# Other start bytes for the pools of on-chip tiles in a hybrid decoder block (short convolution, RG-LRU, MLP)

## The chip, the core and the metric

The kernel runs on one core of a Trainium2 chip. The metric is the device time of one execution in microseconds (us); a lower number is better.

## What is computed

One decoder block over a sequence of 2048 tokens of 1024 features, in fp32:

```
h = rmsnorm(x, norm_mix_g)
u = h @ w_in                                    # 1024 -> 3584 columns
gate_b, gate_c, v, x_r, g = split(u)            # 512, 512, 512, 1024, 1024 columns
y_conv = gate_b * causal_dwconv(gate_c * v, conv_w)         # 3 taps
xr = causal_dwconv(x_r, rnn_conv_w) + rnn_conv_b            # 4 taps
y_rnn = rg_lru(xr, w_a, b_a, w_x, b_x, lru_lambda) * gelu(g)
y = concat(rmsnorm(y_conv, g_norm_conv), rmsnorm(y_rnn, g_norm_rnn))
x = x + y @ w_out                                           # 1536 -> 1024
z = square(relu(rmsnorm(x, norm_mlp_g) @ w_mlp_in))         # 1024 -> 4096
x = x + z @ w_mlp_out                                       # 4096 -> 1024
out = rmsnorm(x, final_norm_g)
```

`rg_lru` makes two sigmoid gates by 64-wide block-diagonal products and runs a linear recurrence along the tokens.

## The kernel before

**Tiling.** The tokens are cut into four blocks of 512 (`TB`), and the features into chunks of 128 partitions. Blocks are handled in pairs: the mixers and the output projection of block 0, then those of block 1, then the MLP of both together; the same again for blocks 2 and 3. The MLP of a pair is done by a scheme with seven products in place of eight (classes `Up` and `Down`, order `ORDER`), whose intermediate `z` tiles are written to device memory and fetched again.

**Products.** Each fp32 operand is split into a high part of type fp32r and the rest, also fp32r: ScalarE casts the high part (`split_into`, L153), VectorE subtracts it (L154). Each product is then three TensorE matmuls: high by high, high by low, low by high. Nearly all matmuls take 128x128 stationary columns and a moving operand of 512 columns. These are the places:

| line | product | stationary operand, its pool | moving operand, its pool | names in the profile |
|---|---|---|---|---|
| L193 | `h @ w_in` | weights, `wp` | h, `hp` | ps_g, ps_x, ps_b, ps_c, ps_v |
| L213 | `y @ w_out` | y, `tp` | weights, `wp` | po |
| L584 | gates of the RG-LRU | gates, `tp` | xr, `tp` | psri |
| L731 | `Up` of the MLP | weights, `wp` | H, `tp` (H1 and H2 in `hp`) | up |
| L845 | `Down` of the MLP | z, `wp` | weights, `wp` | dn |

L420 is the first product of the program, on 256 moving columns. L976 are transposes of 128x128 in fp32 against the identity `ident`.

**Pools.** All tiles lie in SBUF pools, opened in this order:

```
    cp = ctx.enter_context(tc.tile_pool(name="cp", bufs=1))
    hp = ctx.enter_context(tc.tile_pool(name="hp", bufs=2))
    tp = ctx.enter_context(tc.tile_pool(name="tp", bufs=TSLOTS))
    wp = ctx.enter_context(tc.tile_pool(name="wp", bufs=WSLOTS))
    xp = ctx.enter_context(tc.tile_pool(name="xp", bufs=2))
    sp = ctx.enter_context(tc.tile_pool(name="sp", bufs=4))
```

`cp` holds constants and parameters. `hp` has two tiles of 16384 bytes per partition for h. `tp` has 29 general tiles (`TSLOTS`) of 4096 bytes, `wp` 15 tiles (`WSLOTS`) of 4096 bytes for weights and their parts (and for the parts of `z`). `xp` has two tiles of 4128 bytes for `xr_in` and `cv`, the inputs of the convolutions, which take turns. `sp` holds small columns. The pools lie one behind the other in a partition, so the size of `cp` sets where all others begin. Since 4096 and 16384 are multiples of 512, all tiles of a pool lie at the same byte of a 512-byte block; of the two tiles of `xp` the second lies 32 bytes further on.

**Order.** A layer records the instructions and puts them into the queues of the engines with their waits; some stretches are in the order in which they are written (`manual_schedule`). SyncE issues all DMAs. The order does not look at addresses.

Of the kernel before, what the change touches and what calls it, by code (L numbers as in the profile page):

```python
# [8 lines left out]
F32 = mybir.dt.float32  # L9
# [5 lines left out]
P = 128  # L15
# [35 lines left out]
def block_kernel(  # L51
# [31 lines left out]

    cp = ctx.enter_context(tc.tile_pool(name="cp", bufs=1))
    hp = ctx.enter_context(tc.tile_pool(name="hp", bufs=2))
    tp = ctx.enter_context(tc.tile_pool(name="tp", bufs=TSLOTS))
    wp = ctx.enter_context(tc.tile_pool(name="wp", bufs=WSLOTS))
    xp = ctx.enter_context(tc.tile_pool(name="xp", bufs=2))
    sp = ctx.enter_context(tc.tile_pool(name="sp", bufs=4))
# [132 lines left out]
    ident = cp.tile([P, P], F32, name="ident")  # L222
    make_identity(nc, ident)
    ones = cp.tile([P, P], F32, name="ones")
    nc.gpsimd.memset(ones, 1.0)

    xt = {}
# [992 lines left out]
```

## Time and profile before

| | |
|---|---|
| two timed runs | 2209.63 and 2211.41 us, median 2210.52 us |
| the profiled execution, first to last instruction | 2208.7 us |
| so outside the span, against the median | 1.8 us |
| granted TensorE clock, mean | 0.994 of full speed |
| busy share of the span | TensorE 98%, weight loads 81%, VectorE 76%, ScalarE 47%, GpSimd 3% |
| chain that ended last | TensorE 93%, VectorE 4%, DMA 1%, issue on SyncE 1% |

The chain of work that ended last is followed back from the last instruction: at each step to what released it, or to the instruction before it on its engine. The profile's duration of a matmul (about 390 ns) runs from its start to the modelled end of its results; matmuls overlap, so what counts is the distance from one start to the next.

### The profile page before, as it was taken

The numbers are of one execution on the slowest core, as the hardware profiler recorded it, in microseconds if no ns is written. First come the engines' busy times: TensorE is split into PE (matmuls) and PEld (weight loads), VectorE is DVE, ScalarE is ACT, GpSimd is POOL, SyncE is SP. The second block draws the span as 40 slices with busy tenths as digits, with TensorE's granted clock in tenths as the row PEclk, the third lists the DMA queues.
The fourth block names the chain that finished last, engine by engine and source line by source line (L and its number), as shares of the span: only waits on it lengthen the run. The fifth ranks groups of instructions, "written<-read, shape, count | busy, mean of one in ns | idle before, by whom it ended". The sixth has DMA issues, their size and how long they took to land.

```text
span 2208.7 us, 25232 instructions
## 1 busy us (share of the span) xinstructions
PE 2172.8 (98%) x9684; PEld 1799.6 (81%) x9684; DVE 1670.0 (76%) x1948; ACT 1038.2 (47%) x1346; POOL 62.0 (3%) x62
## 2 busy tenths in 40 slices
PE   7999999999999999999999999999999999999997
PEld 6888888887888888888888888888888888788886
DVE  7787677868775778868888776886796665887867
ACT  4864378534332334334568644764443332433343
POOL 3010000000000000000100000010000000000000
PEclk8999999999999999999999999999999999999999
DMA  7334443432444378454162434233334345854432
GB/s 223 103 123 153 140 155 115 144 116 94 162 152 163 131 254 314 141 177 145 51 234 88 157 120 172 77 115 144 124 114 178 127 166 199 301 207 158 133 103 76
DMA packets 180776, 334.10 MB, mean 151 GB/s; under 512 B 14672, under 2 KB 106928, under 8 KB 180656
## 3 DMA queue, kind: packets, MB, share of 16 engines
q1 hardware_dynamic: 180656, 332.49, 44.0%
q8 instruction: 76, 1.25, 0.2%
q14 instruction: 44, 0.36, 0.1%
HBM read 252.76 MB, written 79.69 MB: 151 GB/s over the span
## 4 chain that ended last, share of the span: by engine, by line
PE 93%; DVE 4%; DMA 1%; SPq 1%; issue 0%; ACT 0%; DVEq 0%
PE dn L845 27%; PE up L731 25%; PE po L213 11%; PE ps_g L193 8%; PE ps_x L193 7%; PE ps_b L193 4%; PE ps_c L193 4%; PE ps_v L193 4%; PE psri L584 2%; DVE H L154 1%; PE start_x L420 1%; PE tps L976 1%; DVE w_lo L154 1%; DVE x L889 0%; DMA z<-d_z 0%
## 5 line engine op out<-in xcount | busy, mean ns | idle before, releaser
L731 PE MATMUL up<-H,w_hi 128*128 128x512 f32 x1792 | 553.7, 390 | 2.6 <-ACT w_hi L153 1.9
L731 PEld LDWEIGHTS up<-H,w_hi 128*128 128x128 f32 x1792 | 336.7, 188 | 73.3 <-ACT w_hi L153 2.7
L731 PE MATMUL up<-H,w_lo 128*128 128x512 f32 x896 | 350.0, 391 | 3.2 <-DVE w_lo L154 3.2
L845 PE MATMUL dn<-w_lo,z_hi 128*128 128x512 f32 x896 | 348.9, 389 | 1.9 <-DVE w_lo L154 1.9
L845 PE MATMUL dn<-w_hi,z_hi 128*128 128x512 f32 x896 | 348.8, 389 | 0.0
L845 PE MATMUL dn<-w_hi,z_lo 128*128 128x512 f32 x896 | 348.8, 389 | 0.0
L153 ACT CAST w_hi<-w 128x1024 fp32r<-128x1024 f32 x156 | 164.1, 1052 | 346.0 <-PE up L731 164.8
L154 DVE TENSOR_TENSOR w_lo<-w,w_hi 128x1024 fp32r<-128x1024 f32 x156 | 190.3, 1221 | 119.6 <-PE up L731 43.1
L154 DVE TENSOR_TENSOR w_lo<-raw,w_hi 128x1024 fp32r<-128x1024 f32 x156 | 191.4, 1230 | 99.1 <-ACT w_hi L153 45.4
L153 ACT CAST w_hi<-raw 128x1024 fp32r<-128x1024 f32 x160 | 165.5, 1046 | 103.0 <-PE po L213 67.1
L153 ACT CAST z_hi<-z 128x1024 fp32r<-128x1024 f32 x112 | 117.7, 1051 | 198.8 <-PE dn L845 158.2
L731 PEld LDWEIGHTS up<-H,w_lo 128*128 128x128 f32 x896 | 168.6, 188 | 40.0 <-DVE w_lo L154 4.9
L845 PEld LDWEIGHTS dn<-w_lo,z_hi 128*128 128x128 f32 x896 | 168.2, 188 | 37.5 <-DVE w_lo L154 2.4
L845 PEld LDWEIGHTS dn<-w_hi,z_hi 128*128 128x128 f32 x896 | 168.2, 188 | 34.8
L845 PEld LDWEIGHTS dn<-w_hi,z_lo 128*128 128x128 f32 x896 | 168.2, 188 | 34.7
L154 DVE TENSOR_TENSOR z_lo<-z,z_hi 128x1024 fp32r<-128x1024 f32 x112 | 138.3, 1235 | 56.2 <-issue 26.5
L857 DVE TENSOR_TENSOR x<-dn,x 128x1024 f32<-128x1024 f32 x112 | 136.4, 1219 | 20.9 <-PE dn L845 20.7
L213 PE MATMUL po<-w_hi,y_hi 128*128 128x512 f32 x384 | 119.5, 392 | 0.0
L213 PE MATMUL po<-w_hi,y_lo 128*128 128x512 f32 x384 | 118.4, 389 | 0.0
L213 PE MATMUL po<-w_lo,y_hi 128*128 128x512 f32 x384 | 118.3, 389 | 0.0
L193 PE MATMUL ps_g<-h_hi,w_hi 128*128 128x512 f32 x256 | 99.8, 390 | 0.0
L193 PE MATMUL ps_g<-h_lo,w_hi 128*128 128x512 f32 x256 | 99.7, 389 | 0.0
(222 smaller groups left out, 3569.5 us busy)
## 6 DMA issues: line engine op xcount, KB each, us to landing
raw<-in_w_in_dram SPq DMA_DIRECT2D x112, 512.0 KB, 3.7
z<-d_z SPq DMA_DIRECT2D x112, 512.0 KB, 3.9
w<-in_w_mlp_in_dram SPq DMA_DIRECT2D x64, 512.0 KB, 5.8
d_z<-snap SPq DMA_DIRECT2D x64, 512.0 KB, 3.4
raw<-in_w_out_dram SPq DMA_DIRECT2D x48, 512.0 KB, 3.7
d_z<-z SPq DMA_DIRECT2D x48, 512.0 KB, 4.0
w<-in_w_mlp_out_dram SPq DMA_DIRECT2D x48, 512.0 KB, 3.6
x<-in_x_dram SPq DMA_DIRECT2D x20, 512.0 KB, 8.8
```

The costliest lines, as they stand in the source:

```text
L153: nc.scalar.copy(hi, src)
L154: (lo_engine or V).tensor_tensor(lo, src, hi.bitcast(F32), SUB)
L193: nc.tensor.matmul(ps[:, j, lo:hi], ws[k // 4][:, k % 4, j * P : (j + 1) * P], hs[:, k, lo:hi], start=k == 0 and i == 0, stop=k == KD - 1 ...
L213: nc.tensor.matmul(ps[:, half, :], ys[:, j, t * P : (t + 1) * P], ws[j][:, 0, half * 512 : (half + 1) * 512], start=first and i == 0, stop ...
L420: nc.tensor.matmul(start_x[:, j, 256 * th : 256 * th + 256], w[a][q][:, k, j * P : (j + 1) * P], h[b][:, 4 * q + k, 256 * th : 256 * th + ...
L584: nc.tensor.matmul(pr_[:, half, :], ws[:, c, :], xsrc[:, j, :], start=i == 0, stop=i == len(pl) - 1,)
L731: nc.tensor.matmul(ps[:, j, :], ws[:, k, j * P : (j + 1) * P], hs(k), start=i in (1, 2, 5) and k == 0 and n == 0, stop=k == 3 and n == len ...
L845: nc.tensor.matmul(ps[t // 2][:, t % 2, :], zs[:, p, t * P : (t + 1) * P], ws[:, p, :], start=i in (1, 2, 5) and a == 0 and p == 0 and n == 0,
L857: V.tensor_add(xt[b, th, dh], ps[th], xt[b, th, dh])
L976: nc.tensor.transpose(ps[:, k, :], xs[:, k // 4, k % 4 * P : (k % 4 + 1) * P], ident)
```

## The change

Three pieces of SBUF are put between the pools, and nothing reads or writes them: 32 bytes per partition at `ones` in `cp` (`pad`), 128 bytes between `hp` and `tp`, 256 bytes between `tp` and `wp` (`shift`).

```
     hp = ctx.enter_context(tc.tile_pool(name="hp", bufs=2))
+    shift = [ctx.enter_context(tc.tile_pool(name="shift0", bufs=1))]
     tp = ctx.enter_context(tc.tile_pool(name="tp", bufs=TSLOTS))
+    shift.append(ctx.enter_context(tc.tile_pool(name="shift1", bufs=1)))
     wp = ctx.enter_context(tc.tile_pool(name="wp", bufs=WSLOTS))
...
     ones = cp.tile([P, P], F32, name="ones")
+    cp.tile([P, 8], F32, name="pad")
+    for n, pool in enumerate(shift):
+        pool.tile([P, 32 + 32 * n], F32, name="shift")
     nc.gpsimd.memset(ones, 1.0)
```

What the built programs have as start addresses (bytes in a partition, and the byte within a block of 512):

| tiles | before | after |
|---|---|---|
| `ident`, `ones` | 2176, 2688: 128 | 2176, 2688: 128 |
| `hp`, first tile | 6112: 480 | 6144: 0 |
| `tp`, first tile | 38880: 480 | 39040: 128 |
| `wp`, first tile | 157664: 480 | 158080: 384 |
| `xp`, its two tiles | 219104: 480, 223232: 0 | 219520: 384, 223648: 416 |

The rest of `cp` behind `ones` moves by 32 bytes, `sp` by 416. On each engine the same instructions stand in the same order, with the same waits; no DMA is added, taken away or split in another way. Each tile keeps its slot within its pool. Only the addresses differ.

More of the change, by code (lines that the diff above doesn't have):

```diff
@@ L85, in block_kernel @@
     hp = ctx.enter_context(tc.tile_pool(name="hp", bufs=2))
+    shift = [ctx.enter_context(tc.tile_pool(name="shift0", bufs=1))]
     tp = ctx.enter_context(tc.tile_pool(name="tp", bufs=TSLOTS))
+    shift.append(ctx.enter_context(tc.tile_pool(name="shift1", bufs=1)))
     wp = ctx.enter_context(tc.tile_pool(name="wp", bufs=WSLOTS))
@@ L224, in block_kernel @@
     ones = cp.tile([P, P], F32, name="ones")
+    cp.tile([P, 8], F32, name="pad")
+    for n, pool in enumerate(shift):
+        pool.tile([P, 32 + 32 * n], F32, name="shift")
     nc.gpsimd.memset(ones, 1.0)
```

## Prediction

> **What bounds the kernel now.** First the page: which engine is busy, and what the chain that ended last is made of.
>
> ```profile
> span 2208.7 us, 25232 instructions
> PE 2172.8 (98%) x9684; PEld 1799.6 (81%) x9684; DVE 1670.0 (76%) x1948; ACT 1038.2 (47%) x1346; POOL 62.0 (3%) x62
> GB/s 223 103 123 153 140 155 115 144 116 94 162 152 163 131 254 314 141 177 145 51 234 88 157 120 172 77 115 144 124 114 178 127 166 199 301 207 158 133 103 76
> ...
> PE 93%; DVE 4%; DMA 1%; SPq 1%; issue 0%; ACT 0%; DVEq 0%
> ```
>
> TensorE stands on 93% of the chain. Whether it waits there or streams is told by the chain in order of time (start, length, what):
>
> ```profile
> 190.97 43.52 PE po L213 x192
> ...
> 558.58 250.08 PE up L731 x1102
> 808.66 304.64 PE dn L845 x1344
> ```
>
> The pieces divided by their counts: 43.52/192 = 226.7 ns, 250.08/1102 = 226.9 ns, 304.64/1344 = 226.7 ns from one start to the next. Three places with operands from different pools, one number, over hundreds of matmuls in a row: TensorE streams, and nothing that another engine does in those 598 us moves it. How many matmuls of 512 columns there are:
>
> ```profile
> L731 PE MATMUL up<-H,w_hi 128*128 128x512 f32 x1792 | 553.7, 390 | 2.6 <-ACT w_hi L153 1.9
> L731 PE MATMUL up<-H,w_lo 128*128 128x512 f32 x896 | 350.0, 391 | 3.2 <-DVE w_lo L154 3.2
> L845 PE MATMUL dn<-w_lo,z_hi 128*128 128x512 f32 x896 | 348.9, 389 | 1.9 <-DVE w_lo L154 1.9
> L213 PE MATMUL po<-w_hi,y_hi 128*128 128x512 f32 x384 | 119.5, 392 | 0.0
> L193 PE MATMUL ps_g<-h_hi,w_hi 128*128 128x512 f32 x256 | 99.8, 390 | 0.0
> ...
> L193 PE MATMUL ps_x<-h_hi,w_hi 128*128 128x512 f32 x240 | 93.6, 390 | 0.0
> L193 PE MATMUL ps_c<-h_hi,w_hi 128*128 128x512 f32 x128 | 51.0, 399 | 0.0
> L584 PE MATMUL psri<-xr_lo,gate_hi 128*128 128x512 f32 x64 | 24.9, 389 | 0.0
> ```
>
> Each but the first two is one of three equal passes, and ps_b and ps_v are like ps_c. So: up 2688, dn 2688, po 1152, L193 3 x (256 + 240 + 3 x 128) = 2640, psri 192; together 9360. At 226.7 ns they make 2121.9 us of the 2208.7. What the change does to these 226.7 ns is the whole question: 1 ns of it is 9.4 us.
>
> **What the 226.7 ns are made of.** L420 has matmuls of 256 columns, at half and at full clock; each row is a group of eight, and the distance of the rows' starts counts:
>
> ```profile
> 25.78 1.91 PE L420 MATMUL start_x<-h_hi,w_lo 128*128 128x256 f32 x8
> 27.48 1.63 PE L420 MATMUL start_x<-h_hi,w_hi 128*128 128x256 f32 x8
> ...
> 30.86 1.12 PE L420 MATMUL start_x<-h_hi,w_hi 128*128 128x256 f32 x8
> 31.82 1.12 PE L420 MATMUL start_x<-h_lo,w_hi 128*128 128x256 f32 x8
> 32.78 1.12 PE L420 MATMUL start_x<-h_hi,w_lo 128*128 128x256 f32 x8
> ```
>
> Before the clock rises: 1.70/8 = 213 ns for 256 columns, so 106.5 ns at full clock and 213 ns for 512. After: 0.96/8 = 120 ns. So 256 columns cost 120 and 512 cost 226.7: 106.7 for 256 columns, and 13.3 ns that don't grow with the columns. At half clock the 13.3 ns are not there: they are hidden behind the slower array, so they come from the feeding of operands and not from the array. Feeding operands is reading SBUF, and that is what the change could touch. 13.3 ns x 9360 = 125 us is the end of the range for a gain; for a loss I take the same size, 125 us, for want of a row.
>
> **The change, part by part.** No instruction, wait or DMA comes or goes, so each term is a count times a change of a duration.
>
> *Pads:* nobody reads or writes them, no instruction; 0.
>
> *VectorE:* it stands on 4% of the chain, 88 us. Here the trace has the experiment already: of the two tiles of the pool `xp` one lies at byte 480 and one at byte 0, and they take turns as `xr_in`, while the output `xr` lies at 480. The first row pair read the tile at 0, the second that at 480, the third that at 0:
>
> ```profile
> 271.88 1.02 DVE L541 TENSOR_SCALAR xr<-xr_in,prm 128x512 f32<-128x512 f32 x2
> 272.82 4.05 DVE L550 SCALAR_TENSOR_TENSOR xr<-xr_in,prm,xr 128x512 f32<-128x512 f32 x6
> ...
> 294.53 1.02 DVE L541 TENSOR_SCALAR xr<-xr_in,prm 128x512 f32<-128x512 f32 x2
> 295.47 4.05 DVE L550 SCALAR_TENSOR_TENSOR xr<-xr_in,prm,xr 128x512 f32<-128x512 f32 x6
> ...
> 323.24 4.06 DVE L550 SCALAR_TENSOR_TENSOR xr<-xr_in,prm,xr 128x512 f32<-128x512 f32 x6
> ```
>
> 4.05, 4.05, 4.06 us: neither the byte at which an operand starts nor whether two operands of an instruction start at the same byte is worth 0.01 us in 4. So 0; with 0.25% either way on 88 us, 0.2 us. The rest of VectorE's time lies under TensorE's:
>
> ```profile
> 0.00:37.00 37.00, 22.54 (x128) 20.85 (x129) 24.29 (x45) 18.65 (x35) 12.40 (x16) 0.82 0.73 230
> 495.00:559.00 64.00, 58.95 (x251) 46.83 (x250) 51.59 (x65) 28.08 (x43) 0.00 (x0) 0.97 0.29 101
> 559.00:809.00 250.00, 250.00 (x1105) 207.05 (x1104) 169.43 (x145) 85.02 (x84) 0.00 (x0) 1.00 0.47 168
> 809.00:1113.00 304.00, 304.00 (x1343) 251.81 (x1342) 249.44 (x241) 123.96 (x140) 6.72 (x4) 1.00 0.51 173
> ```
>
> (stretch, its length, then busy us of TensorE, weight loads, VectorE, ScalarE and GpSimd, then the clock, the DMA share and GB/s.) In dn VectorE has 249 of 304 us: that cover is gone only if its instructions get 22% longer. In the start of up (495 to 559) TensorE waits for it, and there the 0.25% count.
>
> *ScalarE and GpSimd:* 0% of the chain; ScalarE has 124 of 304 us in dn, so 0.
>
> *DMAs:* the same packets go to other bytes. On the chain they are these:
>
> ```profile
> 13.37 8.66 DMA raw<-in_w_in_dram
> 22.05 1.32 DMA prow<-in_g_norm_rnn_dram
> ...
> 1865.16 6.09 DMA w_first<-in_w_mlp_out_dram
> 1871.26 9.68 DMA z<-d_z
> ```
>
> 25.8 us. All tiles that DMAs fill or empty lie at 480, so no row shows another byte. Bound: the fastest slice of the page moves 314 GB/s, the start 230; if the new bytes brought 314, 25.8 x (1 - 230/314) = 6.9 us would go, and I allow as much the other way. I take 0, the value that the same packets and sizes give.
>
> *TensorE:* between a gain of 125 and a loss of 125 us. I take 0. The nearest rows are the VectorE pair above: the same memory, read by another engine at 480 and at 0, without a difference. And 226.7 ns hold at up, dn and po alike while VectorE, ScalarE and DMAs are busy for 34% to 82% of the time: if accesses got in each other's way by their addresses, the steps would be ragged, and they are not. Sum: 2208.7 + 0, and with the 1.8 us outside the span 2210.5, the median before. Its own range: 7 us by DMAs, 1 us by the runs shown (2209.63 to 2211.41), 0.2 by VectorE and a little for the shifted waits: 2199 to 2222.
>
> A rule to weigh here: the page "SBUF — State Buffer" of the Trainium skill, section "Specifications (TRN2)", gives SBUF lines of 16 bytes. 480, 0, 128 and 384 are all multiples of 16, so by it no operand reads more lines than before, and the sum stays 0. That would speak against the change doing anything; the pair of `xr_in` agrees, and for TensorE no row here shows it.
>
> **Rivals.**
>
> *1. The start byte is the 13.3 ns (faster).* All starts go from 480, which is no multiple of 64, to multiples of 128. If TensorE's feed fetches in larger pieces, a start inside a piece costs a piece more per operand, whatever the number of columns: exactly the form of the 13.3 ns. For it speaks a row of matmuls whose moving operand, `ident`, lies at byte 128:
>
> ```profile
> 258.86 1.03 PE L976 MATMUL tps<-ident,xs 128*128 128x128 f32 x8
> ```
>
> With 273 ns for the last, (1.03 - 0.27)/7 = 108.6 ns per step; that is 256 columns' time, 106.7 ns, and only 2 more. Against it: this is fp32, with 128 columns in the time of 256, so its feed has twice the time and could hide the 13.3 as the half clock does. Price: 11.3 ns x 9360 = 106 us, 2105 us. Beside that stands a rule of the Trainium skill, page "TensorE: Matmul & The Clock Gate", section "Back-to-back issue gap": 512 columns every N/2.4 + 2.5 = 216 ns. The 226.7 measured here are 11 ns more, so the rule and this trace differ; if the layout were the reason, the sum by the rule would be 9360 x 11, some 100 us less.
>
> *2. Equal bytes are the 13.3 ns (faster, in part).* Weights of the next matmul are loaded while the present one streams. If the two streams collide because both start at 480, only matmuls with operands from different pools gain: up, po and L193, 6480. dn (both `wp`) and psri (both `tp`) stay. 6480 x 11.3 = 73 us, 2137 us. For it: that the 13.3 ns are fixed, as one weight load per matmul is. Against it: the streams move on through the block, so a collision by start byte should depend on when the load begins, and the step never varies.
>
> *3. Different bytes collide (slower).* The mirror of it: equal starts are the good case, and the streams of up, po and L193 now meet. Priced at another 13.3 ns as the only step size that the trace shows: 6480 x 13.3 = 86 us, 2297 us. It decides from 44 us on (2%), that is when those matmuls go beyond 226.7 + 6.8 = 233.5 ns. Against it the same uniform steps.
>
> *4. The change doesn't arrive:* tiles could lie elsewhere than meant. The addresses of the built program are as the change says; so this has no chance of its own, and its time would be the forecast's.
>
> **How the numbers follow.** The evidence for no effect is direct for VectorE, indirect for TensorE, and TensorE is what counts; so the rivals keep a fifth. No effect 0.80, rival 1 0.07, rival 2 0.06, rival 3 0.07. Predicted: 2210 us. The range 2199 to 2222 holds the forecast's 0.80 and leaves out the rivals' 0.20. A difference under 2% is about what a measurement of this kernel can't tell from no change; faster by more: 0.13, within: 0.80, slower by more: 0.07.
>
> **What would show it.** In the profile after: dn over its 1344 matmuls again 304.6 us, up and po at 226.7 ns per step, and the groups of L550 at 4.05 us with `xr_in` at 384 and 416. If dn, up and po all fall to about 215 ns, it is rival 1; if up and po fall and dn stays, rival 2; if up and po exceed 233 ns, rival 3. If the steps stay and the time moves, look at the DMA pieces of the start (8.66 us) and before the second dn (6.09 + 9.68 us). Wrong I am above all if TensorE's feed sees bytes that VectorE's doesn't.

## The result, and the profile after

The changed kernel takes 2230.01 us (two runs, 2229.22 and 2230.80) against 2210.52: 1.009 times as long, with an interval of 1.0073 to 1.0106. That is outside the predicted range of 2199 to 2222. The profiled execution has a span of 2229.0 us, 20.3 us more than before.

The page of the changed kernel, its head and the chain by engine (its lines in the program are two to five further on: L193 is now L195, L213 L215, L550 L555, L731 L736, L845 L850):

```profile
span 2229.0 us, 25232 instructions
PE 2194.4 (98%) x9684; PEld 1799.7 (81%) x9684; DVE 1670.3 (75%) x1948; ACT 1038.7 (47%) x1346; POOL 62.5 (3%) x62
...
PE 94%; DVE 3%; DMA 1%; SPq 1%; issue 0%; ACT 0%; DVEq 0%
```

TensorE is busy 21.6 us longer with the same 9684 matmuls at the same granted clock (0.994); VectorE, ScalarE and DMAs are as before. The chain in order of time says which matmuls (start us, length us, what):

```profile
61.20 11.19 PE ps_g L195 x48
...
194.28 43.57 PE po L215 x192
...
564.97 251.71 PE up L736 x1102
816.68 304.64 PE dn L850 x1344
```

Against that the piece of L193 in the kernel before that the prediction didn't show:

```profile
61.29 10.88 PE ps_g L193 x48
```

dn has the same 304.64 us to the last digit, po 226.9 ns per step. But ps_g goes from 10.88/48 = 226.7 ns to 11.19/48 = 233.1, and up from 250.08 us to 251.71. In this piece of up 240 matmuls read H1 or H2, which lie in `hp`; the 862 others read H tiles of `tp`. Taken from the single starts in the trace, over all of up, the step is 232.9 ns with H1 and H2 and 226.8 with the others. So the slow matmuls are those with the moving operand in `hp` and the weights in `wp`. Of the others only psri moves by more than 0.2 ns, in stretches of 12 between those of L193: from 226.7 to 228.1 ns, 0.3 us in all, although both of its operands lie in `tp`; why is open.

Adding up, for each line, the distances from one start to the next gives the 20.3 us: L193 +16.5; up +2.4 (+4.7 by the longer steps, -2.3 by fewer waits); dn +1.5 (waits); psri and po +0.5; the first product -0.6.

### The profile page after: what moved, and what is told of

Read it like the earlier page. It is cut to its first block, busy times and chain, and to the rows that moved or that the text cites. A ratio compares the mean times of both kernels' runs of the same rounds, so it can differ in the third digit from the quotient of the medians.

```text
span 2229.0 us, 25232 instructions
## 1 busy us (share of the span) xinstructions
PE 2194.4 (98%) x9684; PEld 1799.7 (81%) x9684; DVE 1670.3 (75%) x1948; ACT 1038.7 (47%) x1346; POOL 62.5 (3%) x62
## 4 chain that ended last, share of the span: by engine, by line
PE 94%; DVE 3%; DMA 1%; SPq 1%; issue 0%; ACT 0%; DVEq 0%
PE dn L850 27%; PE up L736 25%; PE po L215 11%; PE ps_g L195 8%; PE ps_x L195 8%; PE ps_b L195 4%; PE ps_v L195 4%; PE ps_c L195 4%; PE psri L589 2%; PE start_x L425 1%; PE tps L981 1%; DVE w_lo L156 0%; DVE H L156 0%; DVE x L894 0%; DMA z<-d_z 0%
## 5 line engine op out<-in xcount | busy, mean ns | idle before, releaser
L736 PE MATMUL up<-H,w_hi 128*128 128x512 f32 x1792 | 555.4, 391 | 2.3 <-ACT w_hi L155 1.9
L736 PEld LDWEIGHTS up<-H,w_hi 128*128 128x128 f32 x1792 | 336.0, 188 | 75.8 <-ACT w_hi L155 2.7
L736 PE MATMUL up<-H,w_lo 128*128 128x512 f32 x896 | 350.6, 391 | 2.8 <-DVE w_lo L156 2.8
L850 PE MATMUL dn<-w_lo,z_hi 128*128 128x512 f32 x896 | 349.3, 390 | 1.9 <-DVE w_lo L156 1.9
L850 PE MATMUL dn<-w_hi,z_lo 128*128 128x512 f32 x896 | 349.3, 390 | 0.0
L850 PE MATMUL dn<-w_hi,z_hi 128*128 128x512 f32 x896 | 349.1, 390 | 0.0
L736 PEld LDWEIGHTS up<-H,w_lo 128*128 128x128 f32 x896 | 168.2, 188 | 40.9 <-DVE w_lo L156 4.5
L850 PEld LDWEIGHTS dn<-w_lo,z_hi 128*128 128x128 f32 x896 | 168.6, 188 | 37.6 <-DVE w_lo L156 2.3
L850 PEld LDWEIGHTS dn<-w_hi,z_hi 128*128 128x128 f32 x896 | 168.6, 188 | 35.1
L850 PEld LDWEIGHTS dn<-w_hi,z_lo 128*128 128x128 f32 x896 | 168.5, 188 | 34.8
L215 PE MATMUL po<-w_hi,y_hi 128*128 128x512 f32 x384 | 119.4, 392 | 0.0
L215 PE MATMUL po<-w_lo,y_hi 128*128 128x512 f32 x384 | 118.5, 390 | 0.0
L215 PE MATMUL po<-w_hi,y_lo 128*128 128x512 f32 x384 | 118.3, 389 | 0.0
L195 PE MATMUL ps_g<-h_hi,w_hi 128*128 128x512 f32 x256 | 101.2, 395 | 0.0
L195 PE MATMUL ps_g<-h_hi,w_lo 128*128 128x512 f32 x256 | 101.1, 395 | 0.0
```

The costliest lines, as they stand in the source:

```text
L195: nc.tensor.matmul(ps[:, j, lo:hi], ws[k // 4][:, k % 4, j * P : (j + 1) * P], hs[:, k, lo:hi], start=k == 0 and i == 0, stop=k == KD - 1 ...
L215: nc.tensor.matmul(ps[:, half, :], ys[:, j, t * P : (t + 1) * P], ws[j][:, 0, half * 512 : (half + 1) * 512], start=first and i == 0, stop ...
L736: nc.tensor.matmul(ps[:, j, :], ws[:, k, j * P : (j + 1) * P], hs(k), start=i in (1, 2, 5) and k == 0 and n == 0, stop=k == 3 and n == len ...
L850: nc.tensor.matmul(ps[t // 2][:, t % 2, :], zs[:, p, t * P : (t + 1) * P], ws[:, p, :], start=i in (1, 2, 5) and a == 0 and p == 0 and n == 0,
```

## The experiments

**1. Is it the byte or the distance?** After the change the slow pair is `hp` at 0 and `wp` at 384. Either a moving operand at a multiple of 512 is slow (theory S), or the distance of the two operands is (theory R). Two kernels part these: one adds the 32 bytes alone, one the 128 and 256 bytes alone.

```
 pad_only, against before:
+    cp.tile([P, 8], F32, name="pad")

 shift_only, against the changed kernel:
-    cp.tile([P, 8], F32, name="pad")
```

pad_only. 

> Only the 32 bytes in cp are added, so all pools lie at byte 0 and all distances are 0. Theory R: nothing changes, 2210 us, all steps at 226.7 ns. Theory S: all 9360 matmuls now start at a multiple of 512; 9360 x 6.3 ns = 59 us more, about 2270 us.

shift_only. 

> The 128 and 256 bytes between the pools without the 32 bytes: hp at 480, tp at 96, wp at 352. All distances between pools are those of the changed kernel, no pool starts at a multiple of 512. Theory R: as the changed kernel, 2230 us, L193 at 233 ns. Theory S: as before, 2210 us.

Measured: pad_only 2208.97 us, 0.9995 times before (0.9985 to 1.0004); shift_only 2229.08 us, 1.0089 times (1.0074 to 1.0104). Of the chain of pad_only, with all pools at byte 0:

```profile
59.62 10.88 PE ps_g L193 x48
...
556.90 250.08 PE up L732 x1102
806.98 304.64 PE dn L846 x1344
```

and of shift_only, with `hp` at 480 as before, but `wp` at 352:

```profile
60.66 11.19 PE ps_g L195 x48
...
564.51 251.71 PE up L735 x1102
816.22 304.64 PE dn L849 x1344
```

These are the pieces of before and of after. With all pools at byte 0 nothing changes, and the distances without the byte bring the loss back: theory S falls, theory R stands, as far as it names the distance. Its reason, that two reads meet, is not shown by these runs.

**2. A map of the distances.** A kernel of its own runs chains of 48 matmuls on one tile:

```
    def run(name, mbyte, rel, n=512, cols=128, count=N):
        ps = psp.tile([P, 512], F32, tag="ps", name=name)
        m0 = mbyte // 4
        s0 = 6144 + ((mbyte + rel) % BLOCK) // 4
        for i in range(count):
            m = m0 + 512 * (i % 8)
            s = s0 + 256 * (i % 8)
            nc.tensor.matmul(ps[:cols, :n], big[:, s : s + cols], big[:, m : m + n], start=True, stop=True)
```

> This kernel leaves the whole block out: it copies x to the output and runs chains of 48 fp32r matmuls (128x128 stationary, 512 moving columns) on one tile, with chosen start bytes. The name of a chain says the byte of the moving operand in a 512-byte block (zero: 0, odd: 96, old: 480) and, by a letter, how far the stationary operand starts behind it (a: 0, b: 32, ... p: 480). Further chains: 64 and 32 stationary columns, and 256 moving columns, at distances 0, 128 and 384. Theory R (the distance of the two start bytes sets the step, because the load of the next weights and the moving operand meet in the memory): the step depends on the letter alone, about 226.7 ns at a and at i (256), about 233 ns at m (384), other letters open; with fewer stationary columns the 13.3 ns shrink. Theory S (a moving operand that starts at a multiple of 512 is slow): about 233 ns in all zero chains, 226.7 ns in all odd and old chains, whatever the letter.

The timeline has one row per chain; the distance of two rows' starts divided by 48 is the step of the first:

```profile
31.76 11.05 PE L40 MATMUL zero_a<-big 128*128 128x512 f32 x48
42.65 11.35 PE L40 MATMUL zero_b<-big 128*128 128x512 f32 x48
53.84 11.36 PE L40 MATMUL zero_c<-big 128*128 128x512 f32 x48
...
120.83 11.05 PE L40 MATMUL zero_i<-big 128*128 128x512 f32 x48
131.72 11.35 PE L40 MATMUL zero_j<-big 128*128 128x512 f32 x48
...
165.35 11.32 PE L40 MATMUL zero_m<-big 128*128 128x512 f32 x48
176.50 11.37 PE L40 MATMUL zero_n<-big 128*128 128x512 f32 x48
187.71 11.16 PE L40 MATMUL zero_o<-big 128*128 128x512 f32 x48
198.70 11.36 PE L40 MATMUL zero_p<-big 128*128 128x512 f32 x48
...
388.08 11.05 PE L40 MATMUL old_a<-big 128*128 128x512 f32 x48
398.98 11.35 PE L40 MATMUL old_b<-big 128*128 128x512 f32 x48
```

Distance 0 (a): 10.89/48 = 226.9 ns; 32 (b): 11.19/48 = 233.1; 256 (i): 226.9; 384 (m): 11.15/48 = 232.3; 448 (o): 10.99/48 = 229.0. The table has the means of the single steps behind the first six of a chain; odd and old chains have the same numbers within 0.3 ns, and distances of 256 to 480 those of 0 to 224:

| distance, bytes | 0 | 32 | 64 | 96 | 128 | 160 | 192 | 224 |
|---|---|---|---|---|---|---|---|---|
| step, ns | 226.7 | 233.4 | 233.4 | 234.4 | 232.4 | 233.4 | 228.8 | 233.3 |

So the period is 256 bytes, the moving operand's byte plays no part at the three places tried, and equal bytes are the good case, not the bad one. One expectation failed, that fewer stationary columns shrink the 13.3 ns:

```profile
566.22 11.21 PE L40 MATMUL cols_half_zero<-big 128*64 128x512 f32 x48
577.27 11.17 PE L40 MATMUL cols_half_plus<-big 128*64 128x512 f32 x48
588.27 11.17 PE L40 MATMUL cols_half_minus<-big 128*64 128x512 f32 x48
```

With 64 stationary columns the step is 230.0 ns at distance 0 and 229.3 at 128 and 384; with 32 it is 231.6, 230.8 and 230.6. So it isn't shorter, the 13.3 ns are not a cost per stationary column, and distance 0 is no better there than the others: that equal bytes are good is shown for 128 stationary columns alone. With 256 moving columns the step is 120.0 ns at distance 0, 128 and 384 alike.

**3. The map against the kernel.** If the map is right, the loss can be moved to other products, and pools can lie apart without any.

```
 distance_moved, against the changed kernel (puts hp at 0, tp at 128, wp at 256):
-        pool.tile([P, 32 + 32 * n], F32, name="shift")
+        pool.tile([P, 32], F32, name="shift")

 distance_256, against pad_only (puts hp at 0, tp at 256, wp at 256):
+    shift = ctx.enter_context(tc.tile_pool(name="shift0", bufs=1))
     tp = ctx.enter_context(tc.tile_pool(name="tp", bufs=TSLOTS))
...
+    shift.tile([P, 64], F32, name="shift")

 all_apart, against the changed kernel (puts hp at 0, tp at 64, wp at 128):
-        pool.tile([P, 32 + 32 * n], F32, name="shift")
+        pool.tile([P, 16], F32, name="shift")
```

distance_moved. 

> hp at byte 0, tp at 128, wp at 256: the 256 bytes between tp and wp become 128. Now L193 and the H1 and H2 products have the distance 256, the other up products (about 1920 matmuls) and po (1152) the distance 128. Theory R with the map's period of 256: L193 falls back to 226.7 ns, up with H in tp and po rise to about 233 ns, 3072 x 6.3 = 19 us, so about 2229 us, the same time as the changed kernel with the loss at other products. If the h pool itself is what costs: 2210 us.

distance_256. 

> hp at byte 0, tp and wp at 256: pools apart, but all distances 0 or 256. Theory R with the period of 256: all steps at 226.7 ns, 2209 to 2211 us as with the pad alone. If any two pools apart cost, or if the period is 512: L193 and up at 0 against 256 slow, 2225 us or more.

all_apart. 

> hp at byte 0, tp at 64, wp at 128: no two pools are 0 or 256 apart. By the map: L193 and up with H1 and H2, 2640 + 768 matmuls at distance 128, 5.7 ns each, 19 us; up with H in tp, 1920 at 64, 6.7 ns each, 13 us; po, 1152 at 448, 2.1 ns each, 2 us; dn and psri nothing. Sum 34 us, about 2245 us. If each of these 6480 matmuls cost 13.3 ns more, as the third rival had it, 2297 us. If the loss is capped at that of the changed kernel: 2230 us.

| kernel | time, us | against before (interval) | expected if the map holds |
|---|---|---|---|
| distance_moved | 2227.32 | 1.0078 (1.0063 to 1.0093) | 2229 |
| distance_256 | 2208.37 | 0.9992 (0.9982 to 1.0001) | 2209 to 2211 |
| all_apart | 2242.14 | 1.0147 (1.0129 to 1.0165) | 2245 |

The chain of distance_moved has L193 back at 226.7 ns and the loss at po (232.4) and up (232.2 over the piece, of which 240 matmuls read H1 or H2 and stay at 227.0):

```profile
60.13 10.88 PE ps_g L195 x48
...
189.89 44.63 PE po L215 x192
...
561.21 255.83 PE up L736 x1102
817.04 304.85 PE dn L850 x1344
```

That of all_apart has it at all three: ps_g 232.3 ns, po 229.0 (the cheaper distance of 448), up 233.4, while dn, with both operands in `wp`, stays:

```profile
60.68 11.15 PE ps_g L195 x48
...
193.35 43.96 PE po L215 x192
...
565.39 257.20 PE up L736 x1102
822.60 304.68 PE dn L850 x1344
```

For all_apart, steps taken from chains of bare matmuls, times the kernel's counts, gave a loss of 34 us; measured are 32.3 (the kernel before took 2209.85 us beside it). distance_256 and pad_only are the fastest seen, but neither is told apart from the kernel before.

**4. How fine, how long, which type.** The same chains with distances in steps of 4 bytes, other lengths, bf16 and fp32.

> This kernel again leaves the block out and runs chains of 48 matmuls (moving operand at byte 0). Chains fine: stationary operand 0, 4, ... 60 bytes behind; below: 4 to 32 bytes ahead; high: 160 to 208 bytes behind. len: 320, 384, 448, 480 moving columns at distance 0 (same) and 128 (apart). bf: the same in bf16. plain: fp32. Theory R1 (two streams meet in memory lines of some width): inside one line of 16 or 32 bytes the distance makes no difference, so fine a to d or a to h stay at 226.7 ns. Theory R2 (the streams run in step, and only exactly equal places in a block of 256 keep out of each other's way): 226.7 ns at distance 0 alone, and steps of about 233 ns from 4 bytes on. If a chain lies below 226.7 ns, there is a better layout than either kernel has. len: the first map had 120.0 ns for 256 columns at any distance and 232.4 for 512 at 128, so the loss should set in somewhere between; no theory says where. bf and plain: if the loss comes from reading twice as many bytes per column as bf16 does, neither depends on the distance.

```profile
32.16 11.05 PE L44 MATMUL fine_a<-big 128*128 128x512 f32 x48
43.05 11.32 PE L44 MATMUL fine_b<-big 128*128 128x512 f32 x48
54.20 11.24 PE L44 MATMUL fine_c<-big 128*128 128x512 f32 x48
...
210.40 11.05 PE L44 MATMUL below_b<-big 128*128 128x512 f32 x48
221.29 11.36 PE L44 MATMUL below_c<-big 128*128 128x512 f32 x48
...
379.82 8.49 PE L44 MATMUL len_e_same<-big 128*128 128x384 f32 x48
388.15 8.61 PE L44 MATMUL len_e_apart<-big 128*128 128x384 f32 x48
396.59 9.89 PE L44 MATMUL len_f_same<-big 128*128 128x448 f32 x48
...
436.95 10.53 PE L44 MATMUL bf_a<-half 128*128 128x512 bf16 x48
447.32 10.52 PE L44 MATMUL bf_b<-half 128*128 128x512 bf16 x48
457.68 10.52 PE L44 MATMUL bf_c<-half 128*128 128x512 bf16 x48
```

Already 4 bytes behind costs (fine_b, 11.15/48 = 232.3 ns), so theory R1, lines of 16 or 32 bytes, falls. 4 bytes ahead costs nothing (below_b, 10.89/48 = 226.9 ns) and 8 bytes ahead costs 6.7 ns, so "at 0 alone" of theory R2 is not exact either. The other fine distances lie between 228.3 and 235.0 ns without an order that I can read. bf16 steps are 215.9 ns and fp32 steps 429.2 at every distance tried (the trace has two such steps for each fp32 matmul of the program). No fp32r chain of 512 columns is below 226.7 ns, so no layout tried has anything to give beyond that of before. By length, at distance 0 and 128: 320 columns 146.7 and 146.7 ns, 384 columns 173.3 and 176.0, 448 columns 202.6 and 204.1, 480 columns 216.6 and 217.8, 512 columns 226.7 and 232.4. The loss of distance 128 sets in between 320 and 384 columns. Distance 0 isn't without loss at every length either: 13.3 ns plus the prediction's 106.7 ns for 256 columns give 200.0 ns for 448 columns and 213.3 for 480, and at distance 0 they take 2.6 and 3.3 ns more. So it is not the distance alone that counts; why 512 columns go free at distance 0 and 448 do not is open.

**5. Whose weights?** While a matmul streams, the weights of the next are loaded: in the first map's zero_a the load's row starts 3 to 4 ns behind the matmul's and takes 188 ns. The last chains alternate their bytes, so that a matmul's own operands are equal and the next one's apart, or the reverse:

```
        run("own_same_next_apart", (0, 128), (0, 128))
        run("own_apart_next_same", (0, 128), (128, 0))
```

> The block is left out; chains of 48 matmuls whose start bytes alternate from one matmul to the next. own_same_next_apart: each matmul's own two operands start at the same byte (0 and 0, then 128 and 128), but the weights loaded while it streams belong to the next one and start 128 away. own_apart_next_same: its own operands are 128 apart, the next one's weights start at the byte of the present moving operand. Theory N (the moving operand meets the load of the next weights): own_same_next_apart near 232 ns, own_apart_next_same 226.7 ns. Theory O (a matmul's own two operands must start alike): the reverse. line_same and line_apart repeat it with 64 bytes (near 233 ns where the distance counts); own_half_next_full is a control at 256 and 0: 226.7 ns in both theories.

```profile
32.75 11.05 PE L38 MATMUL same<-big 128*128 128x512 f32 x48
43.63 11.32 PE L38 MATMUL apart<-big 128*128 128x512 f32 x48
54.79 11.13 PE L38 MATMUL own_same_next_apart<-big 128*128 128x512 f32 x48
65.76 11.20 PE L38 MATMUL own_apart_next_same<-big 128*128 128x512 f32 x48
76.80 11.08 PE L38 MATMUL again_same<-big 128*128 128x512 f32 x48
87.72 11.04 PE L38 MATMUL own_half_next_full<-big 128*128 128x512 f32 x48
98.59 11.28 PE L38 MATMUL line_same<-big 128*128 128x512 f32 x48
109.71 11.27 PE L38 MATMUL line_apart<-big 128*128 128x512 f32 x48
```

same 226.7, apart 232.5, but own_same_next_apart 10.97/48 = 228.5 and own_apart_next_same 11.04/48 = 230.0: both between. With 64 bytes line_same and line_apart are alike, 231.6 and 231.7 by their single steps, where either theory had one of them at 226.7; the control at 256 and 0 is 226.7, as expected. Neither theory holds alone. Which two reads meet, and why equal bytes are good, stays open.

## Why the prediction was wrong, point by point

- **What bounds the kernel: right.** TensorE streams; 9360 matmuls carry the time, and 1 ns of the step is 9.4 us. The 20.3 us are steps that got longer in 3408 of them (2640 of L193, 768 of up with H1 and H2), by 6.3 and 6.1 ns: 16.6 + 4.7 = 21.3 us, less what the waits and the start gave back.
- **TensorE's term, taken as 0: this step failed.** It measured +21. Two reasons were given, and the runs show what each was worth. The `xr_in` pair was read by VectorE; that VectorE doesn't mind the byte was true and is true after the change (4.05 and 4.06 us per group of L555 with `xr_in` at 416 and 384), but it says nothing on TensorE, whose fp32r step depends on where its two operands lie to each other: 226.7 ns at distance 0, 232.4 at 128. And the uniform steps, taken as a sign that no accesses get in each other's way, overlooked that every pair of fp32r operands in the kernel before lay at the same distance, 0: what is the same everywhere can't show as a raggedness.
- **The end for a loss was a guess "for want of a row".** The term's own bounds of 125 us either way held; the range did not carry them, since it took in only the forecast's own case. That is why 2230 lay outside it.
- **Rival 3 had the condition and the sign** (different bytes are slower) at a chance of 0.07; its reason, two streams that meet, stays open. It mis-sized both factors: 13.3 ns against 6.2 on average, and 6480 matmuls against 3408, since `tp` against `wp` is 256 apart, which the map shows to be as good as 0. With all pools truly apart (all_apart) the time was 2242, not 2297.
- **Rivals 1 and 2** fall with pad_only (all bytes at 0, no gain) and with the map (a distance never helps). The 13.3 ns themselves stand at any byte tried and with 64 and 32 stationary columns. That they come from the feeding of operands, as the prediction inferred, no run tests by itself: bf16, with half the bytes, takes 215.9 ns, which fits it, but bf16 may differ in more than its bytes.
- **VectorE, ScalarE, DMA: 0 was right.** VectorE's busy time is 1670.3 against 1670.0 us, the DMA pieces on the chain are 8.90 against 8.66 us at the start and 9.62 against 9.68 before the second dn. In the changed kernel:

```profile
12.27 8.90 DMA raw<-in_w_in_dram
...
1887.72 9.62 DMA z<-d_z
```

- **Within 2%: right** as a class, by 0.9%. But the reason given, that under 2% can't be told from no change, doesn't hold: the interval of 1.0073 to 1.0106 tells 0.9% from none.

A rule beside this: the page "SBUF — State Buffer" of the Trainium skill, section "Specifications (TRN2)", has lines of 16 bytes. All distances of the first map are multiples of 32, so no operand there reads more lines, and the step still rises by 2.1 to 7.7 ns; and of the two chains at 4 bytes, which both start inside a line, only one loses. So the rule doesn't give this loss. The page "TensorE: Matmul & The Clock Gate", section "Step-by-step: what each phase is for", says that loading the next weights takes no read bandwidth from the running matmul, by two read ports. The bf16 chains agree (215.9 ns at every distance). The fp32r chains are hard to fit to it, since there the place of the weights changes the step by up to 8 ns; which reads meet, if any, no run here shows.

## What to carry to other kernels

In a stream of fp32r matmuls of 512 moving and 128 stationary columns, keep the start bytes of stationary and moving operands equal modulo 256. A small tile between two pools can cost 6 ns per matmul, here 1% of the kernel (shift_only); one ahead of all pools moves them together and costs nothing (pad_only). For other shapes, measure: at 64 stationary columns equal bytes gained nothing. A row that tells you an engine is insensitive holds for that engine; where one engine reads two operands at once, measure it by itself: chains of bare matmuls, 653 us of chip time, predicted a kernel's loss of 32 us within 3 us. And where a term rests on a guess for its bound and all the sensitivity lies there, the range has to carry the bound.

## What the runs showed that was not expected

- The step of fp32r matmuls with 512 moving and 128 stationary columns depends on the distance of the two operands modulo 256 bytes: 226.7 ns at 0, up to 234.4 ns at multiples of 32, 235.0 at 28. The moving operand's own byte (0, 96 or 480) plays no part.
- 4 bytes ahead is as good as 0, 4 bytes behind costs 5.7 ns.
- At distance 128 against 0, 256 and 320 columns lose nothing, 384 lose 2.6 ns, 512 lose 5.7 ns; 448 and 480 lose only 1.5 and 1.2, but there distance 0 itself is 2.6 and 3.3 ns above 13.3 ns plus the columns.
- bf16 takes 215.9 ns for 512 columns, fp32r 226.7 at best: 10.8 ns that no layout removed.
- Fewer stationary columns are not faster: at distance 0, 128 columns 226.7, 64 columns 230.0, 32 columns 231.6 ns. With 64 and 32 columns, distance 128 is 0.7 and 0.8 ns shorter than distance 0.
